# A hybrid decoder block on one core: the first weight block cast by two engines with its products in order of terms, five low parts moved from GpSimd to VectorE, and one weight block split without a PSUM copy

## The chip, the cores and the metric

One core of one Trainium2 chip runs the kernel. The time is device microseconds of one execution, the median of three runs. The engines are called by the names of the profile: PE is TensorE (PEld its weight loads), DVE VectorE, ACT ScalarE, POOL GpSimd, SP the engine that issues nearly all DMAs. Each engine works through its own queue in the order in which the program was written; where one needs another's result it waits on a semaphore.

## The reference, cut to what matters

One decoder block on 512 tokens of 2048 channels in float32. Three token mixers share one input projection and one output projection; a gated feed-forward layer follows.

```python
h = rms_norm(x, norm1_g)
proj = h @ w_in                       # 2048 x 3840, split into the three mixers' parts
out_a = dilated_mixture(...)          # 8 heads, three window/dilation patterns
out_b = conformer_conv(...)           # 31 taps along the tokens, layer norm, swish
out_c = band_attention(...)           # 16 query heads, window 128, sinks
x = x + concat([out_a, out_b, out_c]) @ w_out
h2 = rms_norm(x, norm2_g)
x = x + (silu(h2 @ w_gate) * (h2 @ w_up)) @ w_down
```

## The kernel before

**Products in three terms.** The float32 operands are split into a high part, rounded to the format `fp32r` that TensorE multiplies at full pace, and a low part, the rest. A product is then three matmuls: high by high, high by low, low by high (`mm3`, lines 311 to 314). The high part of a weight block is a cast on ScalarE (`wh`), its low part a subtraction on VectorE (`wl`), both written by `split_up_to`. A block, or unit, is 128 partitions by up to 1024 columns; the first unit of the input projection has 512. The units are cut from raw tiles `w` that DMAs fill, and `next_unit` splits two units ahead of the one in use; three buffers each hold the high and the low parts.

**Start.** `xs[k]` is channel block k of the input, `scaled` makes its high part on ScalarE (line 419) and its low part on VectorE (line 420), both called `h` here. The loop over `k` multiplies the four token blocks of `h` by the first four column blocks of `w_in`, into the four banks `in`. Eight matmuls on zeros (`idle<-warm`) stand in front of it. In the loop each token block gets its three terms in a row, so the second matmul of all needs `wl`.

**Attention and the opening of the output projection.** Steps of attention, convolution and normalisation are put off by a number of ticks (`ticks.after`) and so are written between the products. `split_mix` (line 860) makes a mixer row's parts `mh` and `ml` for the output projection; its low part is made on GpSimd for the eight c rows and on VectorE for the a and b rows. `split_rows(k)` is called before row k is used and splits rows k to k+2 if they are there. The rows are used in the order of `ROWS`: c0, c1, c2, c4, c5, c3, c7, c6, then the a and b rows. `first_two` opens the output projection with two output blocks at once, row by row, while the last heads of attention are still in work: `a1e` and `a2e` are their weights, `a1t` transposes of these, `ak` a key block, `mix_a` a finished a row. The PSUM banks of these tiles come from a pool of six, of which `first_two` holds one.

**Feed-forward layer.** Each group of weights (`g1`, `u1`, and so on) is multiplied by a scheme with seven products in place of eight; its raw tiles `21`, `22`, `11`, `12` are added up on GpSimd (line 200) into sums `s`. From the fifth unit of the first group on, `split_up_to` takes another way: ScalarE writes the high part twice, once into a PSUM tile `wn` (line 293) and once into SBUF as `wh` (line 294), and VectorE subtracts `wn`, so that one of its two inputs comes from PSUM (line 295). The pool `high` of these PSUM tiles has two buffers, and the second normalisation (`n2s`, lines 1074 to 1081) holds one of them while the first group is at work. The units of a group are, in order, `s`, `11`, `21`, `s`, `12`, `22`, `s`; the fifth is called block 12 below, after its raw tile.

Of the kernel before, what the change touches and what calls it, by code (L numbers as in the profile page):

```python
# [9 lines left out]
F32 = mybir.dt.float32  # L10
# [5 lines left out]
P = 128  # L16
T = 512
NT = T // P
D = 2048
KT = D // P  # L20
# [28 lines left out]
ROWS = "c0 c1 c2 c4 c5 c3 c7 c6 a0 a1 b2 b1 b0 b3 a2 a3".split()  # L49
# [38 lines left out]
C_G1, C_G2, C_CW, C_CB, C_LG, C_LB, C_QK, C_SINK, C_ALL = 0, 16, 32, 156, 160, 164, 168, 172, 188  # L88
# [34 lines left out]
def kernel(ctx: ExitStack, tc: tile.TileContext, xT, wi, wo, wgu, wd, cst_in, outT):  # L123
    nc = tc.nc
# [20 lines left out]
    def slot(name, dt=F32, cols=T):  # L145
        return sp.tile([P, cols], dt, name=name, tag="s")

    def wide(i, name, dt=F32):
        return xp.tile([P, 2 * T], dt, name=name, tag=f"x{i}")
# [8 lines left out]
    units = [wi[0][:, :T], wi[0][:, T:]] + [wi[u] for u in range(1, 2 * N_IN)]  # L158
# [7 lines left out]
    raws, held = {}, {}  # L166
# [10 lines left out]
    def drop(key):  # L177
        for buf in [b for b, k in held.items() if k == key]:
            held.pop(buf)
        return raws.pop(key)  # L180
# [87 lines left out]
    splits = {}  # L268
    at = {"entry": 0, "split": 0, "use": 0}

    def pump(limit):
        while at["entry"] < len(entries) and len(raws) < limit and entries[at["entry"]][0] not in held:
            buf, key, parts = entries[at["entry"]]
            (part,) = parts
            n = part.shape[-1] * (part.shape[1] if len(part.shape) == 3 else 1)
            t = take(buf, key, n)[:, :n]
            nc.sync.dma_start(t if len(part.shape) == 2 else t.rearrange("p (n c) -> p n c", n=part.shape[1]), part)
            at["entry"] += 1

    def split_up_to(i):  # L280
        while at["split"] <= min(i, len(works) - 1):
            key, last, eng = works[at["split"]]
            t, n = drop(key) if last else raws[key]
            u = at["split"]
            hi = wp.tile([P, 1024], F32R, name=f"wh{u}", tag="hi", bufs=SPLIT_BUFS)
            lo = wp.tile([P, 1024], F32R, name=f"wl{u}", tag="lo", bufs=SPLIT_BUFS)
            if eng or u < len(units) + 4:
                eng = eng or nc.vector
                nc.scalar.copy(hi[:, :n], t[:, :n])  # L289
                eng.tensor_sub(lo[:, :n], t[:, :n], hi[:, :n].bitcast(F32))  # L290
            else:
                near = psum["high"].tile([P, 1024], F32R, name=f"wn{u}", tag="h")
                nc.scalar.copy(near[:, :n], t[:, :n])
                nc.scalar.copy(hi[:, :n], t[:, :n])
                nc.vector.tensor_sub(lo[:, :n], t[:, :n], near[:, :n].bitcast(F32))  # L295
            splits[u] = (hi, lo)
            at["split"] += 1
# [5 lines left out]
    def next_unit(ahead=SPLIT_AHEAD):  # L303
        sums_now()
        u = at["use"]
        at["use"] += 1
        split_up_to(u + ahead)
        pump(RAW_EARLY if u < 20 else RAW_BUFS + N_WIDE)
        return splits.pop(u)

    def mm3(out, wh, wl, xh, xl, start, stop):
        nc.tensor.matmul(out, wh, xh, start=start, stop=False)  # L312
        nc.tensor.matmul(out, wh, xl, start=False, stop=False)  # L313
        nc.tensor.matmul(out, wl, xh, start=False, stop=stop)  # L314
# [4 lines left out]
    xs = []  # L319

    def load_first(k):
        x = slot(f"x{k}")
        nc.sync.dma_start(x, xT[k])
        xs.append(x)

    for k in range(X_AHEAD):
        load_first(k)
        u = k if k < 2 else k // 2 + 1
# [18 lines left out]
    def col(i):  # L347
        return cst[:, i:i + 1]
# [64 lines left out]
    def scaled(x, g, tag, k):  # L413
        if k < N_WIDE:
            both = wide(k, f"{tag}{k}", F32R)
            hi, lo = both[:, :T], both[:, T:]
        else:
            hi, lo = slot(f"{tag}h{k}", F32R), slot(f"{tag}l{k}", F32R)
        nc.scalar.activation(hi, x, AF.Copy, scale=g)
        nc.vector.scalar_tensor_tensor(lo, x, g, hi.bitcast(F32), op0=ALU.mult, op1=ALU.subtract)  # L420
        return hi, lo

    def add_square(acc, x, k, tag, eng=nc.gpsimd):
        if k == 0:
            nc.scalar.activation(acc, x, AF.Square)
        else:
            sq = slot(f"{tag}{k}")
            nc.scalar.activation(sq, x, AF.Square)  # L428
            eng.tensor_add(acc, acc, sq)  # L429
# [11 lines left out]

    g4 = [(column if j < COLUMN_BANKS - 1 else bank)(f"in{j}") for j in range(HEAD4)]
    h_hl = {}
    for k in range(2):
        h_hl[k] = scaled(xs[k], col(C_G1 + k), "h", k)
        split_up_to(k)
    pump(RAW_EARLY)
    add_square(ssum, xs[0], 0, "sq")
    for k in range(KT):
        if k + 2 < KT:  # L450
            h_hl[k + 2] = scaled(xs[k + 2], col(C_G1 + k + 2), "h", k + 2)
        if k < 2 or k % 2 == 0:
            wh, wl = next_unit()
            o = 0
        if k + X_AHEAD < KT:
            load_first(k + X_AHEAD)
        if k == 4:
            nc.sync.dma_start(cst[:, C_G2:], cst_in[:, C_G2:])
        if k + 1 < KT:
            add_square(ssum, xs[k + 1], k + 1, "sq")  # L460
        hi, lo = h_hl.pop(k)
        h_hi.append(hi)
        h_lo.append(lo)
        for i in range(NT):
            s = slice(i * P, (i + 1) * P)
            mm3(g4[i], hi[:, s], lo[:, s], wh[:, o:o + T], wl[:, o:o + T], k == 0, k == KT - 1)
        o += T
    xs = None
    c64 = cp.tile([P, NT], F32, name="c64")
# [79 lines left out]
    def ln_out(mix):  # L549
        b = spread(ln["r"], "lrs")  # L550
        for j in range(NB):
            nc.vector.tensor_mul(yconv[j], yconv[j], b)
        for j in range(NB):
            nc.scalar.activation(yconv[j], yconv[j], AF.Silu, bias=col(C_LB + j), scale=col(C_LG + j))
            mix[f"b{j}"] = yconv[j]
        for n, name in enumerate(r for r in ROWS if r[0] == "b"):
            ticks.after(1 + n, split_mix, name)
# [157 lines left out]
    def attention(kind, box, mix, mi, heads):  # L715
# [7 lines left out]
        def head(h):  # L723
# [107 lines left out]
            def out_rows(b):  # L831
                m = st["mix"]
                nc.vector.tensor_add(m[HALF[h]], m[HALF[h]], b[HALF[h]])
                if h == 1:
                    mix[mi] = m
                    if late:
                        ticks.after(1, split_mix, mi)
# [22 lines left out]
    def split_mix(name):  # L860
        if name not in m_hi:
            m = mix.pop(name)
            hi, lo = slot(f"mh_{name}", F32R), slot(f"ml_{name}", F32R)
            nc.scalar.copy(hi, m)
            (nc.gpsimd if name[0] == "c" else nc.vector).tensor_sub(lo, m, hi.bitcast(F32))  # L865
            m_hi[name], m_lo[name] = hi, lo

    vd = tc.dram_tile([NT, P, T], F32, name="vd")
# [9 lines left out]
    g4 = b = None  # L878
# [14 lines left out]
    for name in PROJ[HEAD4:]:  # L893
        kind, what, j = name[0], name[1], name[2:]
        if name == PROJ[-1]:
            for n, row in enumerate(ROWS[:2]):
                ticks.after(4 + n, split_mix, row)
        b = project(name)
        if kind == "b":
            ticks.after(0, glu if what == "g" else glu_u, int(j), b)  # L900
            continue
        if kind == "c":
            box = Heads(shared) if j else shared
        else:
            box = boxes.setdefault(j, {})
        if what == "k":
            do_k(box, b, name, 1 if kind == "c" else 0)
        elif what == "v":
            do_v(box, b, name)
        else:  # L910
            do_q(box, b, name)
        if what == "q":
            if kind == "a":
                load_v(box, int(j))
                boxes.pop(j)
            attention(kind, box, mix, kind + j, (int(j), int(j) + 8) if kind == "c" else None)
# [88 lines left out]
            operand(q, j, src)  # L1005

    def split_rows(k):
        for name in ROWS[k:k + 3]:
            if name in mix:
                split_mix(name)  # L1010

# [18 lines left out]
    for half in range(2):  # L1030
        for i, n in enumerate(OUT_ORDER[half]):
# [9 lines left out]
            wh, wl = next_unit()  # L1041
            if half == 1 and i == KT - 1:
                drop(first_sum[0][1])
            for kk in range(8):
                if half == 1 and i == KT - 2 and kk == 4:
                    first_sum[0][0]()
                k = 8 * half + kk
# [4 lines left out]
                s = slice(kk * P, (kk + 1) * P)  # L1052
# [345 lines left out]
    for g in range(2 * NP + N_DOWN):  # L1398
        t = g - 2 * NP
        turned = 0 <= t < N_TURNED  # L1400
        if t < 0:
            p, m = GU_ORDER[g // 2], g % 2
# [4 lines left out]
        for i, q in enumerate(ORDER):  # L1407
            sums_now()
            run(evacs)
            for sub in range(BY // 2 if turned else 1):  # L1410
                w = next_unit(SPLIT_AHEAD - (g == 0 and i == 2))
# [124 lines left out]
```

## Time and profile before

| | |
|---|---|
| three runs | 1879.63 us median (1879.41 to 1881.60) |
| the profiled execution | 1879.36 us, span 1877.5 us, TensorE clock granted 1.0 |
| TensorE busy | 1871.7 us in 9848 matmuls |
| VectorE, ScalarE, GpSimd busy | 1454.1, 1343.7 and 1217.0 us |
| memory traffic | 155 GB/s over the span |

The span runs from the first to the last instruction; the time has 1.9 us more around it. A page of the profile gives busy time by engine; a row of the timeline gives start, duration, engine, line, operation, output and inputs with their shapes, and in brackets how long the engine had stood idle before it and what ended that. Matmuls are pipelined, so the starts of two neighbours tell more than their durations: 128x512 matmuls that nothing holds up start 0.23 us apart.

### The profile page before, as it was taken

The page shows a single profiled execution, that of the slowest core. Times are in us where ns is not written, and L with a number is a line of the kernel's source. Part 1 is how long each engine was busy: PE and PEld are TensorE (multiplying, and loading weights), DVE is VectorE, ACT ScalarE, POOL GpSimd, SP SyncE. Part 2 cuts the span into 40 slices and gives each one's busy share as a digit, 9 for nine tenths or more (in the row PEclk, how much of TensorE's full clock was granted, in tenths as well). Part 3 has the DMA queues.
Part 4 walks back from the last instruction along what each step waited for, and adds up shares of the span by engine and source line. Part 5 has one row for each costly group of instructions (what it writes and reads, how often), then busy time and mean ns, then how long its engine had stood idle before and what let it go on. Part 6 is the DMA issues. An engine that isn't in the chain of part 4 may idle for free.

```text
span 1877.5 us, 28557 instructions
## 1 busy us (share of the span) xinstructions
PE 1871.7 (100%) x9848; PEld 1609.1 (86%) x9848; DVE 1454.1 (77%) x2376; ACT 1343.7 (72%) x1883; POOL 1217.0 (65%) x812
## 2 busy tenths in 40 slices
PE   9999999999999999999999999999999999999999
PEld 7888888888888888888888888888888888888888
DVE  7578999897679777777777777777777677778887
ACT  6246655553466887888878888888888887777675
POOL 5023444362155887778878877888787767766786
PEclk9999999999999999999999999999999999999999
DMA  7333233333342354443544445344455475578984
GB/s 271 122 109 102 81 105 102 121 107 138 113 146 89 114 178 142 163 163 132 184 134 164 162 137 181 132 166 160 145 175 196 151 237 185 196 253 283 311 241 124
DMA packets 157986, 301.09 MB, mean 160 GB/s; under 512 B 29968, under 2 KB 69008, under 8 KB 157840
## 3 DMA queue, kind: packets, MB, share of 16 engines
q1 hardware_dynamic: 157696, 299.25, 48.8%
q8 instruction: 78, 1.28, 0.3%
q14 instruction: 68, 0.56, 0.1%
q10 hardware_dynamic: 144, 0.01, 0.0%
HBM read 241.27 MB, written 50.33 MB: 155 GB/s over the span
## 4 chain that ended last, share of the span: by engine, by line
PE 96%; DVE 1%; issue 1%; ACT 1%; POOL 1%; DMA 0%; SPq 0%; DVEq 0%; POOLq 0%; ACTq 0%
PE out L1125 51%; PE out L1267 16%; PE o L313 3%; PE o L314 3%; PE o L312 3%; PE cq L312 1%; PE cq L313 1%; PE cq L314 1%; PE in L313 1%; PE ak L312 1%; PE bg L312 1%; PE ak L314 1%; PE ak L313 1%; PE bu L312 1%; PE bu L314 1%; PE bg L313 1%
## 5 line engine op out<-in xcount | busy, mean ns | idle before, releaser
L1125 PE MATMUL out<-h,wh 128*128 128x512 f32 x2464 | 588.4, 391 | 0.0
L1125 PEld LDWEIGHTS out<-h,wh 128*128 128x128 f32 x2464 | 452.7, 188 | 87.5
L1125 PEld LDWEIGHTS out<-h,wl 128*128 128x128 f32 x2464 | 316.2, 191 | 12.4 <-DVE wl L295 0.4
L1125 PE MATMUL out<-h,wl 128*128 128x256 f32 x2464 | 320.3, 283 | 0.2 <-DVE wl L295 0.2
L1267 PE MATMUL out<-wh,a 128*128 128x512 f32 x896 | 221.3, 389 | 0.0
L1267 PEld LDWEIGHTS out<-wh,a 128*128 128x128 f32 x896 | 168.2, 188 | 34.9
L289 ACT CAST wh<-w 128x1024 fp32r<-128x1024 f32 (+1 forms) x93 | 96.7, 1042 | 125.0 <-PE o L313 43.3
L290 DVE TENSOR_TENSOR wl<-w,wh 128x1024 fp32r<-128x1024 f32 (+1 forms) x93 | 117.2, 1262 | 46.7 <-ACT wh L289 45.7
L1267 PE MATMUL out<-wl,a 128*128 128x512 f32 x448 | 119.7, 389 | 0.0
L1267 PEld LDWEIGHTS out<-wl,a 128*128 128x128 f32 x448 | 84.1, 188 | 17.4
L513 DVE SCALAR_TENSOR_TENSOR y<-bu,cst,y 128x511 f32<-128x511 f32 (+14 forms) x120 | 90.3, 753 | 0.7
L1125 PE MATMUL out<-a,wh 128*128 128x512 f32 x330 | 80.1, 391 | 0.0
L1125 PEld LDWEIGHTS out<-a,wh 128*128 128x128 f32 x330 | 60.2, 188 | 11.4
L312 PE MATMUL o<-mh_c,wh 128*128 128x512 f32 x128 | 51.2, 400 | 0.0
L313 PE MATMUL o<-ml_c,wh 128*128 128x512 f32 x128 | 50.1, 392 | 0.4 <-POOL ml_c L865 0.3
L314 PE MATMUL o<-mh_c,wl 128*128 128x512 f32 x128 | 50.1, 391 | 0.0
L1312 DVE TENSOR_TENSOR Y<-Y,out 128x512 f32<-128x512 f32 x48 | 30.8, 683 | 19.0 <-PE out L1267 18.9
L1125 PEld LDWEIGHTS out<-a,wl 128*128 128x128 f32 x330 | 43.3, 191 | 2.2
L1125 PE MATMUL out<-a,wl 128*128 128x256 f32 x330 | 44.0, 283 | 0.0
L429 POOL TENSOR_TENSOR ssum<-ssum,sq 128x512 f32<-128x512 f32 x15 | 26.6, 1770 | 19.3 <-ACT sq L428 18.8
L312 PE MATMUL cq<-hh,wh 128*128 128x512 f32 x96 | 38.6, 402 | 0.0
L314 PE MATMUL cq<-hh,wl 128*128 128x512 f32 x96 | 37.5, 391 | 0.0
(3111 smaller groups left out, 5197.0 us busy)
## 6 DMA issues: line engine op xcount, KB each, us to landing
od<-a SPq DMA_DIRECT2D x140, 256.0 KB, 4.7
a<-od SPq DMA_DIRECT2D x140, 256.0 KB, 6.2
w<-in_wi SPq DMA_DIRECT2D x59, 512.0 KB, 3.6
w<-in_wo SPq DMA_DIRECT2D x32, 512.0 KB, 3.6
x<-in_xT SPq DMA_DIRECT2D x16, 256.0 KB, 6.7
xr<-in_xT SPq DMA_DIRECT2D x16, 256.0 KB, 3.8
x2d<-xr SPq DMA_DIRECT2D x16, 256.0 KB, 2.0
yd<-z SPq DMA_DIRECT2D x16, 256.0 KB, 5.5
```

The lines of the kernel that those rows point to most:

```text
L289: nc.scalar.copy(hi[:, :n], t[:, :n])
L290: eng.tensor_sub(lo[:, :n], t[:, :n], hi[:, :n].bitcast(F32))
L312: nc.tensor.matmul(out, wh, xh, start=start, stop=False)
L313: nc.tensor.matmul(out, wh, xl, start=False, stop=False)
L314: nc.tensor.matmul(out, wl, xh, start=False, stop=stop)
L429: eng.tensor_add(acc, acc, sq)
L513: nc.vector.scalar_tensor_tensor(yconv[j][:, i:], hconv[j][:, :T - i], c, yconv[j][:, i:], op0=ALU.mult, op1=ALU.add)
L1125: nc.tensor.matmul(out, lhs[:, s], rhs, start=begin, stop=last and low == flip[0] and x is xs[-1], skip_group_check=True)
L1267: nc.tensor.matmul(to[h], x[:, h * P:(h + 1) * P], v[:, j], start=sub == 0 and h not in started, stop=sub == 1 and n in (len(todo) - 1, le ...
L1312: nc.vector.tensor_add(t, t, b)
```

## The change

It has three parts.

1. The first weight unit is cast by two engines: VectorE casts its first 128 columns, ScalarE the other 384, and the subtraction is written behind the low part of the first `h`. The first channel block's twelve matmuls run term by term over the four token blocks: four high by high, four with the low part of `h`, four with the low part of the weights.
2. Of the c rows, GpSimd makes the low parts of rows 3 to 5 of `ROWS` (c4, c5, c3); VectorE makes the other five. `split_rows` looks at four rows instead of three.
3. The way through PSUM begins one unit later: block 12 of `g1` is split from its SBUF cast, as the units before it are.

```diff
@@ split_up_to
-            if eng or u < len(units) + 4:
+            if u == 0:
+                nc.vector.tensor_copy(hi[:, :P], t[:, :P])
+            elif eng or u < len(units) + 5:
                 eng = eng or nc.vector
                 nc.scalar.copy(hi[:, :n], t[:, :n])
                 eng.tensor_sub(lo[:, :n], t[:, :n], hi[:, :n].bitcast(F32))
@@ the start
-    for k in range(2):
-        h_hl[k] = scaled(xs[k], col(C_G1 + k), "h", k)
-        split_up_to(k)
+    t0 = raws[0][0]
+    split_up_to(0)
+    h_hl[0] = scaled(xs[0], col(C_G1), "h", 0)
+    hi, lo = splits[0]
+    nc.scalar.copy(hi[:, P:T], t0[:, P:T])
+    nc.vector.tensor_sub(lo[:, :T], t0[:, :T], hi[:, :T].bitcast(F32))
+    t0 = None
+    h_hl[1] = scaled(xs[1], col(C_G1 + 1), "h", 1)
+    split_up_to(1)
@@ the loop over k
+        if k == 0:
+            for x, w in ((hi, wh), (lo, wh), (hi, wl)):
+                for i in range(NT):
+                    nc.tensor.matmul(g4[i], x[:, i * P:(i + 1) * P], w[:, :T], start=x is hi and w is wh, stop=False)
+            continue
@@ split_mix
-            (nc.gpsimd if name[0] == "c" else nc.vector).tensor_sub(lo, m, hi.bitcast(F32))
+            (nc.gpsimd if name in ROWS[3:6] else nc.vector).tensor_sub(lo, m, hi.bitcast(F32))
@@ split_rows
-        for name in ROWS[k:k + 3]:
+        for name in ROWS[k:k + 4]:
```

The queues show where this puts the instructions. In the rows below the line numbers of the changed kernel are some lines higher than those of the profile (`split_mix`'s subtraction stands in line 865 before and in 878 after); the numbers at the names tell tiles of one name apart.

TensorE's queue at the start, before, behind the matmuls on zeros (`in` is a bank, `wh` and `wl` stand for the weights' parts, `h` for either part of the first activations):

```order
L312 MATMUL in_139<-wh_146,h_143 128x512
L313 MATMUL in_139<-wl_147,h_143 128x512
L314 MATMUL in_139<-wh_146,h_143 128x512
L312 MATMUL in_140<-wh_146,h_143 128x512
L313 MATMUL in_140<-wl_147,h_143 128x512
L314 MATMUL in_140<-wh_146,h_143 128x512
```

The same place in the changed kernel:

```order
L475 MATMUL in_139<-wh_143,h_146 128x512
L475 MATMUL in_140<-wh_143,h_146 128x512
L475 MATMUL in_141<-wh_143,h_146 128x512
L475 MATMUL in_142<-wh_143,h_146 128x512
L475 MATMUL in_139<-wh_143,h_146 128x512
L475 MATMUL in_140<-wh_143,h_146 128x512
L475 MATMUL in_141<-wh_143,h_146 128x512
L475 MATMUL in_142<-wh_143,h_146 128x512
L475 MATMUL in_139<-wl_144,h_146 128x512
L475 MATMUL in_140<-wl_144,h_146 128x512
```

The first matmul with `wl` moved from second to ninth place.

VectorE's queue in the changed kernel in the opening of the output projection, about the rows that free the banks of `ak3t` and `a1o` (before, the same rows stand there without the two of line 878):

```order
L619 TENSOR_TENSOR aq3lo<-aq3raw,aq3hi 128x512
L648 SCALAR_TENSOR_TENSOR ak_4211<-ak3raw,gqk,ak3t 64x512
L648 SCALAR_TENSOR_TENSOR ak_4213<-ak3raw,gqk,ak3t 64x512
L878 TENSOR_TENSOR ml_c_4216<-mix_c_2769,mh_c_4215 128x512
L687 TENSOR_TENSOR av_4199<-av3s,av_4199 128x4x64
L687 TENSOR_TENSOR av_4200<-av3s,av_4200 128x4x64
L846 TENSOR_TENSOR mix_a_4203<-mix_a_4203,a1o_4155 64x512
L878 TENSOR_TENSOR ml_c_4245<-mix_c_3803,mh_c_4244 128x512
```

The low parts of rows c7 and c6 came into VectorE's queue here, the first of them ahead of `mix_a`. Rows c0, c1 and c2 stand 12 to 29 rows further up.

VectorE's queue about block 12, before:

```order
L438 TENSOR_SCALAR n2v<-n2s 128x4
L1133 TENSOR_REDUCE g1r<-out_5955 128x256
L1138 TENSOR_TENSOR g1r<-g1r,out_5953 128x256
L1139 TENSOR_TENSOR g1r<-g1r,out_5953 128x256
L295 TENSOR_TENSOR wl_6086<-w('12', 'g1')_5686,wn_6087 128x1024
L295 TENSOR_TENSOR wl_6092<-w('22', 'g1')_5538,wn_6093 128x1024
```

And in the changed kernel:

```order
L440 TENSOR_SCALAR n2v<-n2s 128x4
L1146 TENSOR_REDUCE g1r<-out_5956 128x256
L1151 TENSOR_TENSOR g1r<-g1r,out_5954 128x256
L1152 TENSOR_TENSOR g1r<-g1r,out_5954 128x256
L292 TENSOR_TENSOR wl_6087<-w('12', 'g1')_5687,wh_6086 128x1024
L297 TENSOR_TENSOR wl_6091<-w('22', 'g1')_5539,wn_6092 128x1024
```

The place is the same; block 12's subtraction now reads `wh` in SBUF, and ScalarE has one cast less ahead of the next block's two.

More of the change, by code (lines that the diff above doesn't have):

```diff
@@ L463 @@
         h_lo.append(lo)
+        if k == 0:
[3 more added lines that the diff above has]
+            continue
         for i in range(NT):
             s = slice(i * P, (i + 1) * P)
-            mm3(g4[i], hi[:, s], lo[:, s], wh[:, o:o + T], wl[:, o:o + T], k == 0, k == KT - 1)
+            mm3(g4[i], hi[:, s], lo[:, s], wh[:, o:o + T], wl[:, o:o + T], False, k == KT - 1)
         o += T
```

## The prediction

> **What bounds the kernel now.** The page comes first, then the waits of TensorE and of its weight loads (who waited for whom: us in total, times, longest), since only a wait on TensorE can be won back here.
>
> ```profile
> span 1877.5 us, 28557 instructions
> PE 1871.7 (100%) x9848; PEld 1609.1 (86%) x9848; DVE 1454.1 (77%) x2376; ACT 1343.7 (72%) x1883; POOL 1217.0 (65%) x812
> ```
>
> ```profile
> PE o L313 <- POOL ml_c L865: 0.3, 1, 0.3
> ...
> PEld o L313 <- POOL ml_c L865: 1.1, 2, 0.7
> PEld in L313 <- DVE wl L290: 1.1, 3, 0.5
> PEld a1t L795 <- PE o L314: 0.5, 1, 0.5
> PEld out L1125 <- DVE wl L295: 0.4, 1, 0.4
> ```
>
> The reader is to see that TensorE is busy for all but 5.8 us of the span, and that it has 9848 products before as after: the change removes none. All waits of the weight loads in these rows add up to 3.1 us, or 0.17% of the span, and the change aims at them: the first `wl` (0.5 of the 1.1), the rows `ml_c` (1.1), `wl` in block 12's neighbourhood (0.4). So even a complete success is smaller than 0.2% of the time (3.8 us), which is about what a measurement of this kernel can tell from no change. The question is which of these waits go, and which come back.
>
> **First weights and first products.** The timeline of the start without the rows between (start us, duration, engine, line, operation, [idle before <- what ended it]):
>
> ```profile
> 5.26 0.50 PE L312 MATMUL in<-wh,h 128*128 128x512 f32 x1
> 5.99 0.50 PE L313 MATMUL in<-wl,h 128*128 128x512 f32 x1 [0.23 <-DVE wl L290]
> 6.67 0.73 ACT L419 ACTIVATE h<-x,cst 128x512 fp32r<-128x512 f32 x1 [1.46 <-DMA x<-in_xT]
> 7.45 0.62 ACT L289 CAST wh<-w 128x512 fp32r<-128x512 f32 x1
> 8.11 0.69 DVE L290 TENSOR_TENSOR wl<-w,wh 128x512 fp32r<-128x512 f32 x1
> 8.88 0.47 PE L313 MATMUL in<-wl,h 128*128 128x512 f32 x1
> 9.40 1.05 ACT L289 CAST wh<-w 128x1024 fp32r<-128x1024 f32 x1 [0.18 <-DMA w<-in_wi]
> 11.76 0.50 PE L313 MATMUL in<-wl,h 128*128 128x512 f32 x1
> ```
>
> ScalarE's cast of 384 columns instead of 512 is worth, by the slope between the rows of 1024 (1.05) and 512 (0.62), 0.11 us: about 0.51. The first product moves from 5.26 to about 5.15. VectorE's cast of 128 columns is in no row; it lies between nothing and the 0.69 of a 512-column subtraction (the row of 8.11), I take 0.2, and it is off the path either way: the low part of `h` is then ready at about 5.6 and is needed by the fifth product at about 6.1, the low part of the weights at 6.3 for the ninth at about 7.0. The stall before 5.99, where the second product now waits for `wl`, goes, and the twelve products of block 0 end about 0.6 us earlier.
>
> What is late next is the second block. Its activations are made at 6.67, when their DMA lands (the 1.46 of idle time is released by it), its weights at 7.45, their low part by 8.80, and the second product of that block starts at 8.88 now. None of this depends on TensorE, and the order of the DMA queue is unchanged. So TensorE stands still in front of 8.88 instead of in front of 5.99. The same holds once more at 11.76, for weights whose cast waited for a DMA until 9.40. I cost the edit at **0**; at its ends 0.1 worse, and 0.7 better (0.11 and the 0.6) if both later waits moved with it.
>
> **Low parts of the c rows.** TensorE, GpSimd and VectorE in the opening of the output projection:
>
> ```profile
> 402.46 0.47 PE L312 MATMUL o<-mh_c,wh 128*128 128x512 f32 x1
> 403.07 0.50 PE L313 MATMUL o<-ml_c,wh 128*128 128x512 f32 x1
> 406.45 0.42 PEld L795 LDWEIGHTS a1t<-ident,a1e 128*128 128x128 f32 x4 [0.53 <-PE o L314]
> 412.56 0.40 PE L312 MATMUL o<-mh_c,wh 128*128 128x512 f32 x1
> 413.25 0.50 PE L313 MATMUL o<-ml_c,wh 128*128 128x512 f32 x1 [0.28 <-POOL ml_c L865]
> ...
> 399.04 2.62 POOL L779 TENSOR_SCALAR a1e<-a1e,a1d 128x512 f32<-128x512 f32 x1
> 401.63 4.43 POOL L865 TENSOR_TENSOR ml_c<-mix_c,mh_c 128x512 fp32r<-128x512 f32 x3
> ...
> 392.93 1.68 DVE L775 SCALAR_TENSOR_TENSOR a1e<-a1e,mult_a 128x384 f32<-128x384 f32 x1
> 399.08 1.22 DVE L290 TENSOR_TENSOR wl<-w,wh 128x1024 fp32r<-128x1024 f32 x1
> 404.21 0.68 DVE L606 TENSOR_TENSOR aq3lo<-aq3raw,aq3hi 128x512 fp32r<-128x512 f32 x1
> 404.81 1.52 DVE L635 SCALAR_TENSOR_TENSOR ak<-ak3raw,gqk,ak3t 64x512 f32<-64x512 f32 x2
> 407.15 0.68 DVE L833 TENSOR_TENSOR mix_a<-mix_a,a1o 64x512 f32<-64x512 f32 x1
> ```
>
> Products of this shape start 0.23 apart. So the wait for the third row's low part (402.46 to 403.07) costs 0.38, with 0.11 of restart behind it; the wait for the eighth row's (412.56 to 413.25) 0.46 and 0.10; and the transposes loaded at 406.45, which take a bank that VectorE's two products into `ak` free at 406.33 (404.81 and 1.52), idle for 0.53 where the weight loads of products 0.23 apart are idle for next to nothing, about 0.3. All three together are 1.35.
>
> VectorE pays five subtractions of about 0.68 (the row of 404.21 has that shape), 3.4 us. It gets something back: a 384-column operation took 1.68 at 392.93, where it met GpSimd's first subtraction, which is gone. Followed by hand from 392: the first two of the added subtractions cost VectorE 1.36 less the 1.0 or more that the 1.68 loses against a 512-column operation's 0.68, so it is 0.1 to 0.4 late at 399, and the third row's low part is ready at about 401, ahead of its need at 402.7. That stall goes, 0.49. GpSimd's three remaining subtractions then stand back to back from about 402.3, as three stand there now from 401.63. VectorE's `ak` products end at about 405.9; TensorE, earlier by 0.49, wants the bank at 405.7, and goes on at about 406.0: together 0.5 gained.
>
> Then the new queue: ahead of `mix_a` (407.15) VectorE now has the low part of the seventh row, and that meets GpSimd's last subtraction (about 405.5 to 406.8). `mix_a` ends at about 408.8 instead of 407.83, and the next transposes need the bank it frees, at 408.3 by TensorE's own time. That takes back about 0.6. The last stall (0.56) goes, as the eighth row's low part is ready some 3 us early. Sum: 0.5 - 0.6 + 0.5, a gain of **0.4**. Ends: all 1.35 gained, or 0.3 lost if VectorE falls a further 1.3 (one GpSimd subtraction) behind at the two banks.
>
> **Block 12 without its PSUM copy.**
>
> ```profile
> 603.78 0.15 DVE L438 TENSOR_SCALAR n2v<-n2s 128x4 f32<-128x4 f32 x1
> ...
> 605.00 2.40 POOL L200 TENSOR_TENSOR w('s', 'g1')_5737<-w('s', 'g1')_5737,w('12', 'g1')_5686 128x1024 f32<-128x1024 f32 x1
> 605.35 1.21 DVE L295 TENSOR_TENSOR wl<-w('12', 'g1')_5686,wn 128x1024 fp32r<-128x1024 f32 x1
> 607.35 2.41 POOL L200 TENSOR_TENSOR w('s', 'u1')_6078<-w('21', 'u1')_5991,w('22', 'u1')_5993 128x1024 f32<-128x1024 f32 x1
> 607.65 1.11 PE L1125 MATMUL out<-h,wl 128*128 128x256 f32 x8
> 608.92 1.22 PE L1125 MATMUL out<-h,wl 128*128 128x256 f32 x8 [0.16 <-DVE wl L295]
> ...
> 577.98 2.41 POOL L200 TENSOR_TENSOR w('21', 'g1')_5483<-w('21', 'g1')_5483,w('11', 'g1')_5585 128x1024 f32<-128x1024 f32 x1
> 578.07 3.39 DVE L290 TENSOR_TENSOR wl<-w,wh 128x1024 fp32r<-128x1024 f32 x1
> ```
>
> The edit frees a PSUM buffer, so the next block's copy no longer waits for it, and the stall before 608.92 (0.3 and 0.1 of restart) loses its cause: 0.42 to gain. But block 12's own subtraction now reads both operands from SBUF. The row of 578.07 has exactly that form, with a GpSimd addition of two tensors begun just before it: it took 3.39, that is until 1.07 after GpSimd was done; GpSimd's next operation was not let in before it. With one operand in PSUM the same subtraction took 1.21 under such an addition (605.35). In the changed kernel the addition still starts at about 605.0 and the subtraction at about 605.4, since both hang on the row of 603.78, GpSimd through a small operation that reads it and VectorE through three rows that follow it in its queue (1.2 and 1.6 us after it). So it should end at 607.40 + 1.07 = 608.5, where it ends at 606.56 now, and TensorE needs it at 607.65. TensorE waits 0.88; its eight products take 1.06; the next block's low part follows on VectorE at about 609.65. Those products then start at 609.67 instead of 608.92: a loss of **0.75**. Ends: 0.42 gained, 0.9 lost.
>
> **Sum.** 0 - 0.4 + 0.75 = 0.35 slower than the profiled execution's 1879.36, so 1879.7; the median of the runs shown, 1879.63, is 0.27 above that execution, hence **1880.0**.
>
> **Rivals.**
> *No collision at block 12.* If VectorE gets there before GpSimd (a margin of only 0.35), the sum is 0 - 0.4 - 0.42 and the time 1878.8; with all of the c rows' stalls won, 1877.9. For it speaks the small margin, against it that both starts hang on one row. Chance 0.25.
> *The start keeps its gain.* 0.7 less, 1879.3: against it stand two DMA landings. Chance 0.05.
> *The second addition gets in first too.* The slower one, a single mechanism: at 607.4 GpSimd's next addition is ready as well. If it goes ahead of VectorE, block 12's subtraction ends at 609.76 + 1.07 = 610.8, TensorE loses 3.1 instead of 0.75, and the time is 1882.3. It decides on who is served at the hand-over; at 580.39, in the row of 578.07, it was VectorE, done 1.07 later. Chance 0.07.
> *GpSimd's scalings block VectorE too.* Then each subtraction moved to VectorE waits out an `a1e` or `a2e` scaling; VectorE is 1.3 late at both banks, the c rows lose about 0.6 instead of gaining 0.4, and the time is 1881.0. Against it: the subtraction of 399.08 started inside the scaling of 399.04 and took its usual 1.22. Chance 0.08. The Trainium skill's page "SBUF — State Buffer" (section "SBUF: two separate sides") gives the rule behind this rival: of a VectorE operation with two SBUF inputs and any GpSimd operation, the first to start holds the shared ports for its whole length and the other is fully blocked; by that rule the time is this rival's, and the trace agrees with it for additions (578.07) but not for scalings (399.08).
>
> **How the numbers follow.** The forecast has the remaining 0.55. Its own range, from the ends of the c rows, is 1879.0 to 1880.7. The first rival reaches down to 1877.9, the scalings' up to 1881.0, and one of the three runs shown was 1881.6 with nothing changed: 1878.0 to 1881.6, which leaves out the 1882.3 and the far end of the first rival. Faster by over 0.2% would need 3.8 us, more than all waits named: 0.02. Slower by as much needs the second addition and a further stall: 0.05. Same: 0.93.
>
> **What would show it.** The first product at about 5.15, no gap before the second, and a gap in front of 8.9 instead. No wait for `ml_c` at 403 and 413, one for VectorE before transposes near 406 and 408. Block 12's subtraction at 3 us instead of 1.2, and about 0.9 of wait on TensorE behind it. The forecast is wrong if that subtraction takes 1.2, or if the products after 12 us all stand earlier by more than 0.2.

## The result, and the profile after

| | before | after |
|---|---|---|
| median of 20 runs each | 1879.26 us (1878.90 to 1881.60) | 1882.68 us (1881.24 to 1885.13) |
| after / before | | 1.0016, 95% interval 1.0011 to 1.0022 |
| the profiled execution | 1879.36 us, span 1877.5 | 1882.61 us, span 1880.8 |

The change makes the kernel 3.4 us slower. The head of the page of the changed kernel (span; busy time of each engine) and TensorE's waits (engine, tile and line that waited, for whom: us in total, times, longest):

```profile
span 1880.8 us, 28560 instructions
...
PE 1872.8 (100%) x9848; PEld 1610.8 (86%) x9848; DVE 1459.0 (78%) x2382; ACT 1342.7 (71%) x1882; POOL 1210.9 (64%) x807
```

```profile
PE a1t L808 <- DVE ak L648: 2.5, 1, 2.5
...
PE out L1138 <- DVE wl L292: 0.7, 1, 0.7
```

TensorE has as many products as before. The waits for `ml_c` are gone from this list, the one for the first `wl` too; in their place stand a wait of 2.5 us for the `ak` products and one of 0.7 for block 12's low part. Where the 3.3 us of span came from can be summed from the starts of TensorE's matmuls: for each pair of neighbours, the interval beyond the usual one for its shape (0.23 us for 128x512). In stretches of 50 us that sum differs by over 0.2 us between the two profiles at three places only: from 0 to 50 us 2.91 before and 2.39 after, from 400 to 450 us 1.78 and 4.70, from 600 to 650 us 0.57 and 1.36. That is -0.5, +2.9 and +0.8: one place for each part of the change.

**The start**, timeline of ScalarE and TensorE (start us, duration, engine, line, operation, [idle before <- what ended it]):

```profile
6.02 0.72 ACT L421 ACTIVATE h<-x,cst 128x512 fp32r<-128x512 f32 x1 [0.93 <-DMA x<-in_xT]
6.75 0.62 ACT L291 CAST wh<-w 128x512 fp32r<-128x512 f32 x1
...
5.15 2.51 PE L475 MATMUL in<-wh,h 128*128 128x512 f32 x8
7.50 1.08 PE L475 MATMUL in<-wl,h 128*128 128x512 f32 x4
8.42 0.39 PE L314 MATMUL in<-wh,h 128*128 128x512 f32 x1
8.64 0.39 PE L315 MATMUL in<-wl,h 128*128 128x512 f32 x1
```

The first product stands at 5.15, eight and four follow without a gap, and the second block follows without one too (8.42, 8.64). Its activations and weights were there 0.65 and 0.70 us earlier than in the profile before (6.67, 7.45).

**The c rows**, GpSimd, VectorE and TensorE:

```profile
398.37 1.58 POOL L792 TENSOR_SCALAR a1e<-a1e,a1d 128x512 f32<-128x512 f32 x1 [0.82 <-DVE a1d L790]
399.91 4.44 POOL L878 TENSOR_TENSOR ml_c<-mix_c,mh_c 128x512 fp32r<-128x512 f32 x3
...
398.53 1.60 DVE L292 TENSOR_TENSOR wl<-w,wh 128x1024 fp32r<-128x1024 f32 x1
400.06 1.77 DVE L878 TENSOR_TENSOR ml_c<-mix_c,mh_c 128x512 fp32r<-128x512 f32 x1
...
402.40 0.60 DVE L766 SCALAR_TENSOR_TENSOR a2d<-a2d,aq2r 128x1 f32<-128x1 f32 x1
...
403.14 1.50 DVE L788 SCALAR_TENSOR_TENSOR a2e<-a2e,mult_a 128x256 f32<-128x256 f32 x1
...
406.24 1.52 DVE L648 SCALAR_TENSOR_TENSOR ak<-ak3raw,gqk,ak3t 64x512 f32<-64x512 f32 x2
...
404.99 0.40 PE L316 MATMUL o<-mh_c,wl 128*128 128x512 f32 x1
407.90 0.63 PE L808 MATMUL a1t<-ident,a1e 128*128 128x128 f32 x4 [2.51 <-DVE ak L648]
...
409.24 0.63 PE L315 MATMUL o<-ml_c,wh 128*128 128x512 f32 x1
409.66 0.63 PE L316 MATMUL o<-mh_c,wl 128*128 128x512 f32 x1
410.09 0.63 PE L314 MATMUL o<-mh_c,wh 128*128 128x512 f32 x1
```

GpSimd, rid of the low parts of c0 and c1, reaches its scaling at 398.37 instead of 399.04, now 0.16 ahead of VectorE's block subtraction, and its three subtractions begin at 399.91 instead of 401.63. Of the VectorE operations beside them, the subtraction of 128x512 takes 1.77 (0.68 elsewhere), the one of 128x1 0.60, the one of 128x256 1.50. In the kernel before, one VectorE operation is caught beside the three subtractions, too, the one of 128x1 (0.16 when nothing holds it up):

```profile
403.10 1.19 DVE L753 SCALAR_TENSOR_TENSOR a2d<-a2d,aq2r 128x1 f32<-128x1 f32 x1
```

The `ak` products end at 407.76 instead of 406.33, and TensorE, which would have taken their bank at 405.2, stands still for 2.5 us. And then it runs slowly: matmuls that nothing holds up start 0.43 apart (409.24, 409.66, 410.09), half the pace. The granted clock is 0.5 from 408.79 to 412.20.

**Block 12**, GpSimd, VectorE, TensorE:

```profile
607.57 2.39 POOL L200 TENSOR_TENSOR w('s', 'g1')_5738<-w('s', 'g1')_5738,w('12', 'g1')_5687 128x1024 f32<-128x1024 f32 x1
609.91 3.38 POOL L200 TENSOR_TENSOR w('s', 'u1')_6079<-w('21', 'u1')_5992,w('22', 'u1')_5994 128x1024 f32<-128x1024 f32 x1
...
607.92 3.12 DVE L292 TENSOR_TENSOR wl<-w('12', 'g1')_5687,wh 128x1024 fp32r<-128x1024 f32 x1
610.96 1.21 DVE L297 TENSOR_TENSOR wl<-w('22', 'g1')_5539,wn 128x1024 fp32r<-128x1024 f32 x1
...
611.09 1.10 PE L1138 MATMUL out<-h,wl 128*128 128x256 f32 x7 [0.71 <-DVE wl L292]
```

The subtraction starts 0.35 behind the addition and takes 3.12, to 1.08 after the addition's end; the next addition then takes 3.38 instead of 2.41.

### The profile page after: what moved, and what is told of

Its sections match the earlier page's. It is cut to its first block, busy times and chain, and to the rows that moved or that the text cites. A ratio compares the mean times of both kernels' runs of the same rounds, so it can differ in the third digit from the quotient of the medians.

```text
span 1880.8 us, 28560 instructions
## 1 busy us (share of the span) xinstructions
PE 1872.8 (100%) x9848; PEld 1610.8 (86%) x9848; DVE 1459.0 (78%) x2382; ACT 1342.7 (71%) x1882; POOL 1210.9 (64%) x807
## 4 chain that ended last, share of the span: by engine, by line
PE 96%; DVE 3%; issue 0%; ACT 0%; POOL 0%; DVEq 0%; ACTq 0%; POOLq 0%
PE out L1138 51%; PE out L1280 16%; PE o L314 3%; PE o L316 3%; PE o L315 3%; PE cq L314 1%; PE cq L315 1%; PE cq L316 1%; PE ak L314 1%; PE ak L316 1%; PE bg L314 1%; PE ak L315 1%; PE bu L314 1%; PE bg L316 1%; PE bg L315 1%; PE bu L316 1%
```

## The experiments

All are edits of the kernel before, whose lines they name. Two theories for the c rows were put against each other: **shared access** (GpSimd's subtractions hold up VectorE operations that read two inputs from SBUF) and **load** (VectorE has too much work ahead of the `ak` products). Times are medians of 11 runs, beside runs of the kernel before on the same chip.

**Each part by itself.** The first: the start's hunks of the diff shown above, nothing else.

> The first part alone (first weights cast by two engines, first products in order of terms). Forecast on record: 0, the first product at about 5.15 us and the 0.5 us given back as standstill in front of 8.9. Rival, from the changed kernel's trace (second block's activations made at 6.02 and weights at 6.75, not 6.67 and 7.45): the gain is kept, -0.5 us, and the two transfers land early in this profile as well. If they land early in some executions and late in others, whatever the kernel, the profiles of the other three kernels of this group, whose start is the old one, show both times as well, and the median moves by something between 0 and -0.5.

Measured: 1879.11 us against 1879.29, ratio 0.9999 (0.9990 to 1.0007). ScalarE and TensorE of this run:

```profile
6.46 0.72 ACT L421 ACTIVATE h<-x,cst 128x512 fp32r<-128x512 f32 x1 [1.62 <-DMA x<-in_xT]
7.11 0.62 ACT L291 CAST wh<-w 128x512 fp32r<-128x512 f32 x1
...
8.37 0.39 PE L314 MATMUL in<-wh,h 128*128 128x512 f32 x1
8.63 0.50 PE L315 MATMUL in<-wl,h 128*128 128x512 f32 x1
```

The second product of the second block stands at 8.63 where it stood at 8.88, and a little of the forecast standstill is there: the third follows at 8.97, so the two intervals are 0.14 over the usual 0.23 each. The transfers' times change from execution to execution: over all profiles of this study, whatever the start, the second block's weight cast begins between 6.75 and 7.77. Part of the gain is kept, 0.2 us by the medians, and the interval holds both no gain and a full one.

The second part:

```diff
-            (nc.gpsimd if name[0] == "c" else nc.vector).tensor_sub(lo, m, hi.bitcast(F32))
+            (nc.gpsimd if name in ROWS[3:6] else nc.vector).tensor_sub(lo, m, hi.bitcast(F32))
-        for name in ROWS[k:k + 3]:
+        for name in ROWS[k:k + 4]:
```

> The second part alone (GpSimd makes the low parts of c4, c5 and c3, VectorE those of the other five c rows, four rows looked at). Forecast on record: -0.4 us. From the changed kernel's trace: +2.9 to +3.4 us, with a wait of TensorE for the key block ak of about 2.5 us near 407.5, then about eight matmuls at half pace (0.43 apart for 0.23). Both later theories, shared access to SBUF and too much work on VectorE, say the same of this run; it is the base for the last run of this group. If the loss came from the three parts together, this run is within 1 us of the kernel before.

Measured: 1882.35 us, ratio 1.0015 (1.0006 to 1.0023), 3.06 above the kernel before. The wait is there again (2.5), and so is the half pace behind it. This part carries the loss.

The third part:

```diff
-            if eng or u < len(units) + 4:
+            if eng or u < len(units) + 5:
```

> The third part alone (block 12 split from its SBUF cast). Forecast on record: +0.75 us, block 12's subtraction ends about 1 us after the GpSimd addition beside it (3 us long) and TensorE waits about 0.9 for it. Rival: no collision, the subtraction takes 1.2 and the time is 0.4 below the kernel before.

Measured: 1880.25 us, ratio 1.0005 (0.9996 to 1.0014), 0.96 above. By the starts of the matmuls from 600 to 650 us it costs 0.8 (1.34 against 0.57). GpSimd and VectorE:

```profile
605.31 2.40 POOL L200 TENSOR_TENSOR w('s', 'g1')_5737<-w('s', 'g1')_5737,w('12', 'g1')_5686 128x1024 f32<-128x1024 f32 x1
...
605.66 3.13 DVE L290 TENSOR_TENSOR wl<-w('12', 'g1')_5686,wh 128x1024 fp32r<-128x1024 f32 x1
```

The collision stands as forecast, at the forecast size.

**Shared access or load.** More work for VectorE, none for GpSimd:

```diff
-            (nc.gpsimd if name[0] == "c" else nc.vector).tensor_sub(lo, m, hi.bitcast(F32))
+            (nc.gpsimd if False else nc.vector).tensor_sub(lo, m, hi.bitcast(F32))
-        for name in ROWS[k:k + 3]:
+        for name in ROWS[k:k + 4]:
```

> Second part, but VectorE makes the low parts of all eight c rows and GpSimd none (four rows looked at). Theory 1, shared access: the ak products are late because GpSimd's three subtractions in a row each shut out a VectorE operation with two SBUF inputs. Without them the four operations that were drawn out (1.60, 1.77, 0.60, 1.50) take 1.22, 0.68, 0.16, 0.42, 3.0 us less; three more subtractions cost 3 x 0.61 = 1.8. So the ak products end about 1.1 us EARLIER than in the changed kernel, TensorE's wait there is about 1.4 in place of 2.5, and the time is 1 us or more below the run with the second part alone (about 1881). Theory 2, VectorE has too much work there: three more subtractions make the ak products 1.8 us LATER, the wait is about 4.3 and the time about 1884.5.

Measured: 1879.75 us, ratio 1.0003 (0.9994 to 1.0012), 2.6 below the second part alone, with three more subtractions on VectorE. VectorE and TensorE:

```profile
399.43 1.61 DVE L290 TENSOR_TENSOR wl<-w,wh 128x1024 fp32r<-128x1024 f32 x1
400.97 1.28 DVE L865 TENSOR_TENSOR ml_c<-mix_c,mh_c 128x512 fp32r<-128x512 f32 x2
...
402.82 0.16 DVE L753 SCALAR_TENSOR_TENSOR a2d<-a2d,aq2r 128x1 f32<-128x1 f32 x1
...
404.31 0.42 DVE L775 SCALAR_TENSOR_TENSOR a2e<-a2e,mult_a 128x256 f32<-128x256 f32 x1
...
407.97 0.63 PE L795 MATMUL a1t<-ident,a1e 128*128 128x128 f32 x4 [1.68 <-DVE ak L635]
```

The three operations have their usual times again, only the block subtraction, which meets the scaling, still takes 1.61; the wait shrinks from 2.5 to 1.7 and the half pace is gone. Load alone falls: it wanted a longer wait and 1884.5. Load is not nothing either: with nearly no collision the added subtractions still leave a wait of 1.7, given back nearly whole by the stalls that went.

The same engines for the same low parts, only the look-ahead left at three rows (the first line of the second part's edit, without the second):

> Second part alone, but three rows looked at instead of four: the same engines make the same low parts. Up to the ak products VectorE has exactly the work of the second part alone (c0, c1 and c2); GpSimd has two subtractions in a row behind its scaling instead of three, the third comes behind two later scalings. Theory 1, shared access to SBUF: one collision less, the 256-column operation that took 1.50 takes 0.42, the ak products end about 1.1 us earlier, TensorE waits about 1.4 instead of 2.5 there, no clock drop behind it, about 1880 us. Theory 2, VectorE has too much work there: the ak products end as late as with the second part alone (wait 2.5, about 1882.3).

Measured: 1879.63 us, ratio 1.0001 (0.9993 to 1.0010). VectorE, GpSimd, TensorE:

```profile
401.00 0.68 DVE L865 TENSOR_TENSOR ml_c<-mix_c,mh_c 128x512 fp32r<-128x512 f32 x1
...
402.98 1.52 DVE L775 SCALAR_TENSOR_TENSOR a2e<-a2e,mult_a 128x256 f32<-128x256 f32 x1
...
401.08 3.14 POOL L865 TENSOR_TENSOR ml_c<-mix_c,mh_c 128x512 fp32r<-128x512 f32 x2 [0.19 <-ACT mh_c L864]
...
407.99 0.63 PE L795 MATMUL a1t<-ident,a1e 128*128 128x128 f32 x4 [1.67 <-DVE ak L635]
```

One collision less it is, 1.1 us less on VectorE, and the time follows; but it is another operation than expected. The first GpSimd subtraction now starts 0.08 behind VectorE's (401.08, 401.00), waiting for ScalarE, and VectorE goes through in 0.68; the 128x256 operation is still caught. A look-ahead of one row, with no work moved from engine to engine, is worth 2.8 us (3.06 above the kernel before, against 0.25).

Only the two rows that TensorE waited for:

```diff
-            (nc.gpsimd if name[0] == "c" else nc.vector).tensor_sub(lo, m, hi.bitcast(F32))
+            (nc.gpsimd if name[0] == "c" and name not in ("c2", "c6") else nc.vector).tensor_sub(lo, m, hi.bitcast(F32))
-        for name in ROWS[k:k + 3]:
+        for name in ROWS[k:k + 4]:
```

> Only c2 and c6, the two rows whose low parts TensorE waited for, go to VectorE; the other six stay on GpSimd; four rows looked at. Shared access: GpSimd comes to its scaling as late as in the kernel before (it still has c0 and c1 ahead of it), so VectorE's block subtraction keeps its 1.2 and GpSimd's three subtractions start at about 401.6, not 399.9; ak is 0.3 to 0.6 late, TensorE waits about 1.1 there, both ml_c waits (0.49 and 0.56) are gone: 1878.9 to 1879.6. Too much work: as that, since VectorE gets 0.6 more. A result above 1880.5 speaks against both.

Measured: 1880.67 us, ratio 1.0008 (0.9999 to 1.0017): a miss. VectorE:

```profile
400.52 1.10 DVE L865 TENSOR_TENSOR ml_c<-mix_c,mh_c 128x512 fp32r<-128x512 f32 x1
...
402.19 1.04 DVE L753 SCALAR_TENSOR_TENSOR a2d<-a2d,aq2r 128x1 f32<-128x1 f32 x1
...
403.37 1.50 DVE L775 SCALAR_TENSOR_TENSOR a2e<-a2e,mult_a 128x256 f32<-128x256 f32 x1
```

The block subtraction kept its 1.2, as expected, but c2's, pushed into the stretch, made the operations behind it meet GpSimd: 0.42, 0.88 and 1.08 are lost, 2.4 together, and TensorE waits 2.0 instead of the expected 1.1. The mechanism is that of shared access; where it strikes can't be carried over from one order to another.

**The half pace.** Two and one spare subtractions behind c3's, with all eight low parts on VectorE:

```diff
             nc.scalar.copy(hi, m)
...
+            for _ in range(2 if name == "c3" else 0):
+                nc.vector.tensor_sub(lo, m, hi.bitcast(F32))
             m_hi[name], m_lo[name] = hi, lo
```

> All eight low parts on VectorE, and c3's subtraction made three times with the same result (two spare ones, 1.2 us of VectorE, no GpSimd subtraction anywhere near). It asks for the price of the length of TensorE's wait by itself: the wait for ak grows from 1.7 to 2.9. If the half pace behind the wait comes from the length of the wait (clock theory), the time grows by 1.2 + about 1.2 over the run without the spares, to about 1882.2, and the matmuls behind it stand 0.43 apart. If the half pace needs the collisions (rival), it grows by 1.2 alone, to 1881.0.

> All eight low parts on VectorE and c3's subtraction made twice (one spare one, 0.6 us). The wait for ak is about 2.3 to 2.4, between the 2.0 that left the pace whole and the 2.5 that halved it in most executions. If a length of about 2.5 decides, the time is 0.7 above the run without a spare (1880.4) in most executions; if any wait over 2.0 does it, 1.9 above (1881.6).

Measured with two: 1882.96 us, ratio 1.0018 (1.0010 to 1.0027), 3.58 above the kernel before, where the run without spares was 0.46 above: 3.1 more; the wait is 3.1, and the matmuls behind it stand 0.43 apart with no collision but the scaling's near. So the half pace needs no collisions; a long wait is enough. It cost 0.7 more than expected: the wait grew by 1.46 instead of 1.2 (the spares took 1.42), and by the starts of the matmuls the half pace itself costs 1.5. Measured with one (`range(1 ...`): 1881.00 us, ratio 1.0010 (1.0001 to 1.0019), wait 2.4. The runs fall into two groups, seven from 1880.31 to 1881.05 with the full clock granted and four from 1882.01 to 1882.25 with 0.999. Neither expectation holds for all runs: it happens in some.

**Block 12 the other way round.** GpSimd held back by a spare small operation, so that VectorE is first:

```diff
         n2["r"] = token_scale(ssum2, D, "n2", n2["b"][:, :NT])[1]
+        spare = small("spare")
+        for _ in range(1):
+            nc.gpsimd.tensor_tensor(spare, n2["r"], nhalf[:, :NT], op=ALU.pow)
```

> Third part alone, with one spare small operation of GpSimd (1.0 us) behind its small operation in the second normalisation, so that its addition starts about 1 us later than block 12's subtraction instead of 0.35 earlier. Shared access: the subtraction takes 1.2 instead of 3.1, TensorE's wait for it (0.7 of 0.9) goes, the time is 0.4 below the kernel before and 1.2 below the third part alone (about 1878.9), unless GpSimd's later additions are then late for the second group (then a new wait on POOL). Rival: the subtraction is long for another reason (reading wh and w) and stays at 3, about 1880.2.

Measured: 1880.36 us, ratio 1.0005 (0.9996 to 1.0014), 0.98 above the kernel before. VectorE, GpSimd, TensorE:

```profile
605.24 1.22 DVE L290 TENSOR_TENSOR wl<-w('12', 'g1')_5686,wh 128x1024 fp32r<-128x1024 f32 x1
...
605.96 2.76 POOL L200 TENSOR_TENSOR w('s', 'g1')_5737<-w('s', 'g1')_5737,w('12', 'g1')_5686 128x1024 f32<-128x1024 f32 x1
...
618.23 2.11 PE L1128 MATMUL out<-h,wh 128*128 128x512 f32 x8 [1.23 <-ACT wh L294]
```

The subtraction takes 1.22, so it was the shared access, and TensorE's wait for it is gone. But GpSimd's additions are now 1.3 late (the third starts at 611.15, in the kernel before at 609.84), ScalarE's casts for the second group hang on them, and TensorE waits 1.2 at 618. In the third part alone these additions are as late (611.13), since the second takes 3.38 there; but TensorE, held up at block 12 already, comes to the same place 0.3 after the cast is done. The third part loses about as much in either order.

**Towards a faster version.** The start as in the change; c6 alone on VectorE; block 12 as before:

```diff
-            (nc.gpsimd if name[0] == "c" else nc.vector).tensor_sub(lo, m, hi.bitcast(F32))
+            (nc.gpsimd if name[0] == "c" and name != "c6" else nc.vector).tensor_sub(lo, m, hi.bitcast(F32))
```

> A version meant to beat both kernels: the first part as it is, of the second part only c6 (its low part on VectorE, all other c rows on GpSimd, three rows looked at), without the third part. Shared access and VectorE's queue: c6's subtraction falls behind the ak products and mix_a, where VectorE had stood idle for 0.64 and GpSimd has no three subtractions in a row, so the wait at 413 (0.56) goes and nothing else moves; with 0.2 of the start 1878.6. If too much work on VectorE were the rule, the row after it would be late and the gain lost (1879.3).

Measured: 1878.98 us against 1879.50, ratio 0.9997 (0.9988 to 1.0006). Its slowest run (1879.16) is 2 us below the fastest of the changed kernel; that it is faster than the kernel before is what the medians say, and the interval doesn't settle it. The same with c2 brought forward on GpSimd:

```diff
-            for n, row in enumerate(ROWS[:2]):
-                ticks.after(4 + n, split_mix, row)
+            for n, row in enumerate(ROWS[:3]):
+                ticks.after(3 + n, split_mix, row)
```

> As the run before it, and c0, c1 and c2 split earlier, all three on GpSimd: c0 and c1 one tick sooner and c2 a tick behind c1, ahead of GpSimd's scaling of 399.04 instead of behind it. c2's wait (0.49) goes without work for VectorE, and GpSimd has two subtractions in a row behind the scaling, not three. TensorE then wants the bank of the ak products 0.49 sooner: if they still end at 406.3, the 0.49 is waited for there and the time equals the run before; if one collision less makes them earlier, up to 0.8 below it (1877.8 to 1878.6).

Measured: 1880.34 us, ratio 1.0004 (0.9996 to 1.0013): worse, outside what was expected. TensorE's waits, VectorE and GpSimd:

```profile
PE a1t L808 <- DVE mix_a L846: 1.0, 1, 1.0
PE a1t L808 <- DVE ak L648: 0.8, 1, 0.8
```

```profile
406.58 2.86 DVE L687 TENSOR_TENSOR av<-av3s,av 128x256 fp32r<-128x256 f32 x2
...
406.45 2.71 POOL L878 TENSOR_TENSOR ml_c<-mix_c,mh_c 128x512 fp32r<-128x512 f32 x2
```

The collision moved on: two small subtractions that took 0.76 before take 2.86, and `mix_a` behind them is 2 us late. And c6 by itself, without the start's edit:

> Only c6's low part on VectorE, nothing else changed. With the start's edit as well the median was 0.52 below the kernel before. The waits say 0.56 less 0.16 for a shorter new wait at 411, so -0.4 here, and what is left of the 0.52, about 0.1 to 0.2, is the start's share (alone it measured 0.18). If the start were worth nothing, this run equals the one with both (-0.5); if it kept its whole gain, this run is at 0.

Measured: 1879.40 us against 1879.24, ratio 0.9999 (0.9990 to 1.0008). In the profile the matmuls from 400 to 450 us gain 0.3 (1.50 against 1.78); the runs lie in two clumps (1878.68 to 1879.04, 1879.40 to 1879.55) with one at 1881.07, so the median says little. How the half microsecond divides between start and c6 stays open.

## Why the prediction was wrong, step by step

It said 1880.0, within 1878.0 to 1881.6; it was 1882.68. That the difference stays within 0.2% holds by the median (1.0016, interval to 1.0022), the size doesn't. What made the time wrong is the term of the c rows and a cost that the sum left out, the half pace; by the medians the start and block 12 were off by about 0.2 each. The three parts measured alone add up to 3.84, the whole change to 3.42.

- **What bounds the kernel** was read rightly: the time moved in the three places named and nowhere else, in waits of TensorE and in the half pace behind one of them.
- **Start**, forecast 0 with an end at -0.7: the first product at 5.15 and no gap before the second came as said, the standstill before 8.9 did not. That it was 5.15 is partly luck: it stands at 5.02 to 5.15 in the four profiles with the new start and at 5.02 to 5.48 in the ten with the old one. The step that failed is that the second block's 6.67, 7.45 and 8.80 were taken as fixed because "none of this depends on TensorE". They don't depend on TensorE, but one execution's DMA landings are a sample: they spread by 1 us over the profiles here. Its size, about -0.2 by the medians, lies between the two ends.
- **c rows**, forecast -0.4, measured +3.06 alone: the step that failed is "GpSimd's three remaining subtractions then stand back to back from about 402.3". They began at 399.91. The forecast worked out new times for VectorE's queue and let GpSimd's stay about where it was. In the kernel before GpSimd works without a gap up to its scaling; rid of the two subtractions ahead of it, it has been idle for 0.82, starts the scaling as soon as VectorE's `a1d` is ready, and is no longer held by VectorE's block subtraction there (1.58 instead of 2.62). That is 1.04 of the 1.72 by which the run of three came earlier; 0.54 is the shift of the whole profile (VectorE's rows near 389 stand that much earlier), so of the 0.67 by which GpSimd came sooner to its scaling little is its own.
- **The `ak` products**, the sum's next step: forecast to end at 405.9, they ended at 407.76. Four VectorE operations were drawn out, by 0.38, 1.09, 0.44 and 1.08, 3.0 together. An end at 405.9 has room for none, and needs what the kernel before loses in this way to go: 2.35, at 392.93 (1.13), 397.10 (0.19) and 403.10 (1.03). That went, and the four came in its place. So nothing paid for the three added subtractions ahead of `ak`, 1.8 us of work: counted from the block subtraction of 390.97 (390.44 in the changed kernel), the `ak` products end after 17.32 us instead of 15.36. The upper end of the term, "a further 1.3 (one GpSimd subtraction) behind at the two banks", allowed for one collision where there were several. The stalls for c2 and c6 went as forecast; `mix_a`'s, forecast at 0.6, was covered by the longer one.
- **No price for the half pace**: the sum took a wait to cost its own length. The second part's 3.06 comes apart like this: 0.46 for the run with all eight low parts on VectorE, which has more work there and nearly no collision, 0.8 for the wait that grows from 1.7 to 2.5, and 1.4 for the half pace, which is what parts the changed kernel's 14 runs with a clock of 0.999 (median 1882.87) from its 6 with 1.0 (1881.51). That makes 2.7; 0.4 is left over and not accounted for (the medians of the kernel before differ by up to 0.3 between the groups of runs). Even the executions without half pace (1881.24 to 1881.76) lie at the upper end of the range, three of the six above it.
- **Block 12**, forecast +0.75, measured +0.8 in the profiles and +0.96 alone: right in place, mechanism and size. The gain of 0.42 that stood at the other end isn't to be had by serving VectorE first either.
- **Rivals**: "the second addition gets in first too" didn't come about, VectorE was served at the hand-over and it was the second addition that waited (3.38). "GpSimd's scalings block VectorE too" came about in small: no subtraction that was moved waited out a scaling, but the block subtraction, which takes 1.21 or 1.22 in the seven profiles where it starts 0.04 or 0.05 behind the scaling, takes 1.60 or 1.61 in the six where it starts 0.15 or 0.16 behind, and 1.70 in the one where it starts 0.06 behind. That is a loss of 0.4 or 0.5, not of 1.3. The Trainium skill's page "SBUF — State Buffer" (section "SBUF: two separate sides") would have the later operation fully blocked where the one on GpSimd reads SBUF, as all of these do. The prediction's "any GpSimd operation" is wider than that. For additions and subtractions the runs agree in both orders (3.13 behind an addition, 1.22 ahead of one that then takes 2.76); behind the scaling of 1.58 a full block would have meant 1.42 + 1.22 = 2.6, and 1.60 was measured.

## What to carry to other kernels

Taking work off an engine can move what stands behind it forward, even past another engine's operation: before pricing an edit, write out the new start times of both engines that share an access, not only those of the engine that gets the work. Collisions between two queues depend on tenths of a microsecond of order, so a count of them read from one order can't be carried to another; the look-ahead of one row decided more here than which engine made five low parts. And a wait of TensorE of 2 us or more should be priced above its length.

## What the runs showed of the hardware

How often TensorE fell to half pace by the length of its wait (the wait from each profile, the runs by granted clock, below 1.0 or not):

| wait, us | kernels | runs below 1.0 |
|---|---|---|
| 1.7 | all on VectorE; look-ahead of three | 0 of 22 |
| 2.0 | only c2 and c6 | 3 of 11 |
| 2.4 | one spare | 4 of 11 |
| 2.5 | the changed kernel; the second part alone | 24 of 31 |
| 3.1 | two spares | 10 of 11 |

The chance grows with the wait, without a sharp limit. The profiles show what else counts: where the wait lies. The granted clock changes in steps. In the profile of the changed kernel it is 0.5 for 3.413 us, and the full clock before that lasted 402.77 us, 118 times as long; in the profiles that kept it, the full clock lasted 1870.50 or 1873.92 us, 548 or 549 times as long. So cut into stretches of 3.413 us, counted from the moment at the start at which the clock became full, the waits lie like this:

| profile | wait, us | TensorE idle within a stretch, us | granted clock in the next |
|---|---|---|---|
| all on VectorE | 1.68 | 1.68 (405.60 to 409.01) | 1.0 |
| only c2 and c6 | 2.00 | 0.56 (403.37 to 406.78), then 1.45 | 1.0 |
| one spare | 2.40 | 0.57 (403.40 to 406.82), then 1.83 | 1.0 |
| the changed kernel | 2.51 | 2.51 (405.37 to 408.79) | 0.5 |
| the second part alone | 2.52 | 2.52 (404.83 to 408.25) | 0.5 |
| two spares | 3.14 | 3.07 (405.34 to 408.75) | 0.5 |

An idle time of 1.83 within one stretch left the clock full, 2.51 halved it for the next one, which costs 1.5. A wait that a boundary cuts in two can get away. That this makes the shares of the first table is argued: of the runs without a profile the place of the wait isn't known. The Trainium skill's page "TensorE: Matmul & The Clock Gate" (section "Part 1: The HAM clock gate") has the clock halved after at least one idle window of about 3.4 us that runs freely. The traces agree with a free-running window of that length (3.413); they don't agree that it has to be idle throughout, since 2.51 was enough.

The start scatters from execution to execution, too. Matmuls on zeros stand ahead of the first product, yet the clock becomes full at 5.26 us in the profile of the kernel before and as late as 7.53 in another, and the transfers land at other times (above). The excess of the first 50 us goes from 2.64 to 3.28 in the ten profiles with the old start (3.0 in the mean) and from 2.39 to 2.89 in the four with the new one (2.7). Which share is the clock's and which the transfers' is not separated. An edit worth a few tenths there can't be told by one profile.
